# Second feed-forward of an encoder block: chunks 5 and 8 move from plain token chunks into block-product pairs

## The chip, the cores and the metric

The kernel runs on one core of one Trainium2 chip. Its time is the device time of one execution in microseconds (us). The core's engines run side by side, each with its own in-order queue: TensorE (PE in the profile, its weight loads PEld), VectorE (DVE), ScalarE (ACT), GpSimd (POOL) and SyncE (SP). SP and POOL issue the transfers of this case.

## The reference

The block works on 256 tokens of width 1024 in float32: a feed-forward, a mixer of two branches (a gated recurrence and an attention), a read of a memory of 256 tokens, and a second feed-forward. Only the second feed-forward is touched:

```python
D_MODEL, SEQ, D_FF = 1024, 256, 2816

def swiglu(h, w_in, w_down):
    gate, up = jnp.split(h @ w_in, 2, axis=-1)
    return (jax.nn.silu(gate) * up) @ w_down

h = rmsnorm(x, ffn2_pre_g[l])
x = x + 0.5 * rmsnorm(swiglu(h, ffn2_w_in[l], ffn2_w_down[l]), ffn2_post_g[l])
```

## The kernel before, in words

**Splitting.** Every float32 matrix product is made of three products of reduced-precision parts. A block of weights (128 partitions x 1024 elements, 512 KB, "a weight block" below) is loaded by SP into a `raw` buffer. ScalarE casts it to the reduced type (`hi`, line 153 or 173), VectorE subtracts to get the rest (`lo`, line 155 or 174), and TensorE sums hi x hi, hi x lo and lo x hi. There are four `raw` buffers, four buffers of the tag `extra` (the tiles `sraw`), and eight each of `hi` and `lo`.

**Chunks.** `ffn` cuts the 2816 hidden columns into 11 chunks (0 to 10) of 256; with gate and up a chunk has 512 columns and four weight blocks. The 256 tokens are two halves of 128. A token chunk (`act_tok`) multiplies each half of the tokens with the four blocks: 24 matmuls of 128x512 a half, 48 a chunk, and eight instructions of split work on VectorE and ScalarE (four casts, four subtractions).

**Pairs.** `act_pair` takes two neighbouring chunks c and c+1 as a 2x2 block product (two token halves, two halves of the contraction, two chunks) and computes it with seven block products of 12 matmuls in place of eight. The sums of the token blocks are made once (`pair_inputs`, tiles `sx`). The weight sums are made per pair. In order, the products are: W00 (tile `sums`); then `sums` + W01 (tile `both`); then `sums` + W11; then W11 alone (tile `raw`); then `both` = W01 + W11; then W10 alone; last `sums` + W10. Here Wkn is the half k of the contraction and the chunk c+1-n, and each is two weight blocks, so a pair makes 14 casts and 14 `lo` subtractions. The sums on VectorE are `add` (line 596, two instructions a sum, three sums). The fourth sum, W01 + W11, is made by an accumulating transfer that POOL issues (line 569), for the pairs named in `FETCHED`. Two PSUM banks (`b1`, `b4`) gather several products each, and ScalarE copies intermediate states out (`vw` at line 617, `pc` at 630, `vw` at 638, `pc` at 648). VectorE combines them into the four results (`c01` 645, `c11` 651, `c00` 661, the last straight from the bank), each followed by ScalarE's silu (`sg`, 450) and VectorE's product (`at`, 453 or 455).

**Down products.** The results are transposed on TensorE (line 445, four transposes a chunk), split into `act`, and multiplied with two weight blocks of the second matrix (`down`, 12 matmuls a token half, 24 a chunk), summed over all chunks in four banks (`acc`). Pairs take the down products of earlier chunks between their own products; the last three chunks' down products (8, 9, 10) stand at the end, 72 matmuls:

```python
downs = [(i, h) for i in range(done, min(c, NFF - STAG - 1)) for h in range(2)]   # NFF = 11, STAG = 3
...
while done < (NFF - STAG if last == NFF - 1 else min(c - 1 - (c + 1 in pairs), NFF - STAG - 1)):
```

**Order.** The tables at the head of the file say which chunks are token chunks (`TOKS`), where pairs begin (`PAIRS`) and which pairs use the accumulating transfer (`FETCHED`). In the second feed-forward chunks 0 and 1 come first, then 2 as a token chunk, the pair 3-4, token chunk 5, the pair 6-7, token chunk 8, and the pair 9-10. A framework's scheduler puts the program into one in-order list per engine, and sets the waits. The first feed-forward has the pairs 4-5 and 6-7 next to each other, then token chunk 8 and the pair 9-10. When two pairs follow each other, the casts and subtractions for the second product of the later one are held until the last silu of the earlier (`last_silu`).

Of the kernel before, what the change touches and what calls it, by code (L numbers as in the profile page):

```python
# [32 lines left out]

STAG = 3

TOKS = {"f1_in": (3, 8), "f2_in": (2, 5, 8)}

PAIRS = {"f1_in": (4, 6, 9), "f2_in": (3, 6, 9)}

L_ACT = 21  # L40
L_F1 = 24
# [11 lines left out]
M_T = (103, 115)  # L53
M_O = (126, 130)

FETCHED = {"f1_in": (4, 6, 9), "f2_in": (3, 6, 9)}
R_AT = (66, 130, 188, 252, 286, 332)

FG = 3
# [26 lines left out]
def block_kernel(ctx: ExitStack, tc: tile.TileContext, wts, head_in, gf_in, x_in, mem_in, memT_in, cols, rows, fbias, masks, out):  # L86
# [340 lines left out]
    def ffn(w_in, w_dn, X, r2, n_tok, i_row, first_half, second_half=None):  # L427
# [20 lines left out]
        def act_evac(ps, c, h, r=None, q=None):  # L448
            sg = sp.tile([P, FC], F32, tag="c1", name=nm("sg"), bufs=7)
            silu = S.activation(sg, ps[:, :FC], AF.Silu, scale=r2[h] if r is None else r).ins  # L450
            a = sp.tile([P, FC], F32, tag="c1", name=nm("at"), bufs=7)
            if q is None:
                v = V.tensor_tensor(out=a, in0=ps[:, FC:], in1=sg, op=ALU.mult)
            else:
                v = V.scalar_tensor_tensor(out=a, in0=ps[:, FC:], scalar=q, in1=sg, op0=ALU.mult, op1=ALU.mult)
            evs.append((silu, v.ins))
            ats[c, h] = a
            if h == 1:
                late.append(c)
            return silu  # L460
# [110 lines left out]
        def act_pair(c, between):  # L571
            sx, q, more_parts = pairs_in

            def of(n):
                return lambda kk: (sx[n][:, 0, kk], sx[n][:, 1, kk])
# [4 lines left out]
            def splits(t):  # L580
                u = []
                for r in t:
                    p = parts_of()
                    split(p[0], p[1], r)
                    u.append(p)
                return u
# [7 lines left out]
            def add(t, o):  # L594
                for x, y in zip(t, o):
                    V.tensor_tensor(out=x, in0=x, in1=y, op=ALU.add)  # L596

            def product(ps, stat, u, start):
                for kk in range(4):
                    ah, al = stat(kk)  # L600
                    wh, wl = blk(u, kk)
                    for i, (x, y) in enumerate(((ah, wh), (ah, wl), (al, wh))):
                        MM(ps, x, y, start=start and kk == 0 and i == 0, stop=kk == 3 and i == 2, skip_group_check=not start)
# [16 lines left out]
            add(sums, both)  # L620
            if c in FETCHED[w_in]:
                for j in range(2):
# [17 lines left out]
            product(b4, of("baed"), splits(raw), False)  # L640
            if c not in FETCHED[w_in]:
                add(both, raw)
# [43 lines left out]
        last_silu = []  # L686
        pairs, pairs_in = PAIRS[w_in], None
        for c in range(n_tok):
# [25 lines left out]
        for c in range(n_tok, NFF):  # L714
# [17 lines left out]
            elif c == 2 and first_half:  # L732
                n = len(log)
                (outs,) = act_first((c,), mm)
                for h in range(2):
                    flush(n + L_ACT + 24 * h)
                    act_evac(outs[h], c, h)
            elif c in TOKS[w_in]:
                n = len(log)
# [1073 lines left out]
```

## Time and profile before

| | |
|---|---|
| time, median of 3 runs (range) | 767.17 us (767.07 to 767.82) |
| the profiled execution | 767.82 us |
| its span, first to last instruction | 765.6 us |
| first product of the pair 3-4 to the last of the pair 9-10 | about 618 to 736 us |
| down products of the chunks 8, 9, 10 | about 742 to 759 us |

In the rows, a window's line gives the stretch (us from the span's start), its length, each engine's busy time with its count of instructions, TensorE's granted clock, the DMA engines' busy share and GB/s. A row of a timeline gives start and duration in us, engine, line, operation, tiles (output, arrow, inputs), the count of merged instructions, and in brackets the idle time before and what ended it. "SPq" is SP's queue.

### The profile page before, as it was taken

The page shows a single profiled execution, that of the slowest core. Times are in us where ns is not written, and L with a number is a line of the kernel's source. Part 1 is how long each engine was busy: PE and PEld are TensorE (multiplying, and loading weights), DVE is VectorE, ACT ScalarE, POOL GpSimd, SP SyncE. Part 2 cuts the span into 40 slices and gives each one's busy share as a digit, 9 for nine tenths or more (in the row PEclk, how much of TensorE's full clock was granted, in tenths as well). Part 3 has the DMA queues.
Part 4 walks back from the last instruction along what each step waited for, and adds up shares of the span by engine and source line. Part 5 has one row for each costly group of instructions (what it writes and reads, how often), then busy time and mean ns, then how long its engine had stood idle before and what let it go on. Part 6 is the DMA issues. An engine that isn't in the chain of part 4 may idle for free.

```text
span 765.6 us, 11756 instructions
## 1 busy us (share of the span) xinstructions
PE 756.7 (99%) x4302; PEld 642.8 (84%) x4302; DVE 664.4 (87%) x982; ACT 521.2 (68%) x841; POOL 33.0 (4%) x56
## 2 busy tenths in 40 slices
PE   9999999999999999999999999999999999999996
PEld 8888888888888998898888888888887888888885
DVE  6799998988678898888689899999979899997973
ACT  8667576688774659667666755875968566675762
POOL 0000000000000100200001000001000100000000
PEclk9999999999999999999999999999999999999999
DMA  9778777674745545835668955586386837868641
GB/s 350 235 259 245 214 239 275 182 252 167 233 158 149 185 137 183 284 128 182 189 220 245 267 183 186 175 286 131 114 291 191 257 108 257 236 222 269 176 131 55
DMA packets 47146, 157.88 MB, mean 206 GB/s; under 512 B 5385, under 2 KB 9105, under 8 KB 47089
## 3 DMA queue, kind: packets, MB, share of 16 engines
q1 hardware_dynamic: 43168, 144.83, 55.5%
q0 software_dynamic: 3488, 11.94, 8.7%
q8 instruction: 33, 0.54, 0.3%
q10 hardware_dynamic: 432, 0.37, 0.2%
q14 instruction: 25, 0.20, 0.1%
HBM read 156.06 MB, written 1.06 MB: 205 GB/s over the span
## 4 chain that ended last, share of the span: by engine, by line
PE 85%; DVE 8%; ACT 2%; DMA 2%; issue 1%; DVEq 0%; ACTq 0%
PE mm L100 45%; PE acc L100 33%; PE tr L100 5%; DVE lo L155 2%; DMA raw<-in_wts_dram 2%; PE tr L445 1%; DVE lo L174 1%; ACT hi L153 1%; PE tr L385 1%; DVE xs L421 1%; DVE sraw L1393 1%; DMA head<-in_head_dram 0%; DVE post L416 0%; DVE sx L174 0%; DVE qm L1578 0%
## 5 line engine op out<-in xcount | busy, mean ns | idle before, releaser
L155 DVE TENSOR_TENSOR lo<-raw,hi 128x1024 fp32r<-128x1024 f32 (+1 forms) x188 | 222.3, 1199 | 29.5 <-ACT hi L153 26.2
L153 ACT CAST hi<-raw 128x1024 fp32r<-128x1024 f32 (+1 forms) x188 | 190.9, 1033 | 50.3 <-DMA raw<-in_wts_dram 29.7
L100 PE MATMUL mm<-hi,hlT 128*128 128x512 f32 (+1 forms) x632 | 191.6, 382 | 0.0
L100 PEld LDWEIGHTS mm<-hi,hlT 128*128 128x128 f32 x632 | 116.7, 188 | 20.2
L100 PE MATMUL mm<-lo,hlT 128*128 128x512 f32 (+1 forms) x316 | 119.1, 381 | 0.0
L100 PE MATMUL acc<-hi,act 128*128 128x512 f32 x352 | 113.6, 390 | 0.0
L173 ACT CAST hi<-sraw 128x1024 fp32r<-128x1024 f32 x80 | 83.3, 1052 | 33.9 <-DVE sraw L596 15.6
L174 DVE TENSOR_TENSOR lo<-sraw,hi 128x1024 fp32r<-128x1024 f32 x80 | 96.1, 1221 | 3.8 <-ACT hi L173 3.4
L100 PE MATMUL mm<-hi,sx 128*128 128x512 f32 x280 | 90.8, 391 | 0.0
L100 PEld LDWEIGHTS acc<-hi,act 128*128 128x128 f32 x352 | 66.2, 188 | 13.4
L100 PE MATMUL acc<-lo,act 128*128 128x512 f32 x176 | 69.5, 395 | 0.0
L100 PEld LDWEIGHTS mm<-lo,hlT 128*128 128x128 f32 x316 | 59.3, 188 | 10.0
L100 PEld LDWEIGHTS mm<-hi,sx 128*128 128x128 f32 x280 | 52.5, 188 | 10.9
L100 PE MATMUL acc<-hlT,hi 128*128 128x512 f32 x240 | 60.7, 394 | 0.0
L100 PE MATMUL mm<-lo,sx 128*128 128x512 f32 x140 | 54.9, 392 | 0.0
L100 PEld LDWEIGHTS acc<-hlT,hi 128*128 128x128 f32 x240 | 43.1, 189 | 7.7 <-DVE hlT L373 0.2
L174 DVE TENSOR_TENSOR lo<-raw,hi 128x1024 fp32r<-128x1024 f32 x32 | 38.6, 1221 | 2.1 <-ACT hi L173 2.0
L173 ACT CAST hi<-raw 128x1024 fp32r<-128x1024 f32 x32 | 33.1, 1053 | 8.5 <-issue 3.1
L100 PEld LDWEIGHTS acc<-lo,act 128*128 128x128 f32 x176 | 33.1, 188 | 6.4
L100 PE MATMUL acc<-lo,hT 128*128 128x512 f32 x96 | 37.8, 393 | 0.0
L100 PE MATMUL acc<-hi,hT 128*128 128x512 f32 x96 | 37.7, 392 | 0.1
L100 PE MATMUL acc<-hi,lT 128*128 128x512 f32 x96 | 37.3, 391 | 0.0
(329 smaller groups left out, 1232.4 us busy)
## 6 DMA issues: line engine op xcount, KB each, us to landing
raw<-in_wts_dram SPq DMA_DIRECT2D x215, 512.0 KB, 4.6
sraw<-in_wts_dram SPq DMA_DIRECT2D x32, 512.0 KB, 6.6
sraw<-in_wts_dram POOLq DMA_DIRECT2D x20, 512.0 KB, 5.9
raw<-in_gf_dram SPq DMA_DIRECT2D x12, 344.0 KB, 3.7
head<-in_head_dram SPq DMA_DIRECT2D x7, 392.0 KB, 6.4
grow<-in_rows_dram SPq DMA_DIRECT2D x4, 512.0 KB, 7.6
xs<-in_x_dram SPq DMA_DIRECT2D x2, 512.0 KB, 7.6
cb<-cd POOLq DMA_DIRECT2D x2, 512.0 KB, 4.9
```

The lines of the kernel that those rows point to most:

```text
L100: log.append(PE.matmul(*args, **kw).ins)
L153: casts.append(S.copy(h, r).ins)
L155: los.append(V.tensor_tensor(out=l, in0=r, in1=h.bitcast(F32), op=ALU.subtract).ins)
L173: a = S.copy(hi, src)
L174: b = V.tensor_tensor(out=lo, in0=src, in1=hi.bitcast(F32), op=ALU.subtract)
L385: PE.transpose(blocks[-1][1], src(kb), ident)
L421: summed = V.scalar_tensor_tensor(out=xh, in0=ts[a // 512][:, a % 512 : (b - 1) % 512 + 1], scalar=r, in1=xh, op0=ALU.mult, op1=ALU.add)
L445: PE.transpose(trv[:, j, h * P : (h + 1) * P], ats[c, h][:, j * P : (j + 1) * P], ident)
L1393: V.tensor_tensor(out=x, in0=x, in1=y, op=ALU.add)
```

## The change

Three entries of the tables change, all for the second feed-forward:

```diff
-TOKS = {"f1_in": (3, 8), "f2_in": (2, 5, 8)}
+TOKS = {"f1_in": (3, 8), "f2_in": (2,)}

-PAIRS = {"f1_in": (4, 6, 9), "f2_in": (3, 6, 9)}
+PAIRS = {"f1_in": (4, 6, 9), "f2_in": (3, 5, 7, 9)}
...
-FETCHED = {"f1_in": (4, 6, 9), "f2_in": (3, 6, 9)}
+FETCHED = {"f1_in": (4, 6, 9), "f2_in": (3, 5, 7, 9)}
```

Chunks 3 to 10 become the pairs 3-4, 5-6, 7-8, 9-10, one right behind the other. Two token chunks (96 matmuls, eight casts and eight `lo` subtractions) go; one pair (84 matmuls, 14 casts, 14 subtractions, six adds, three combinations, two accumulating transfers) comes. Through `downs` the down products are dealt out anew: chunks 3 and 4 go into the pair 5-6, chunks 5 and 6 into the pair 7-8, and none into the pair 9-10, which had chunk 6 before.

VectorE, last pair: the rows between the `lo` subtractions of the fifth product and those of the last (before: the last product's two, `lo_1606` and `lo_1608`, stand ahead of `c01`). Before:

```order
L174 TENSOR_TENSOR lo_1606_7571<-sraw_1550_7354,hi_1605_7570 128x1024
L174 TENSOR_TENSOR lo_1608_7575<-sraw_1551_7356,hi_1607_7574 128x1024
L155 TENSOR_TENSOR lo_1614_7604<-raw_1612_7602,hi_1613_7603 128x1024
L645 TENSOR_TENSOR c01_1585_7504<-mm_1569_7416,vw_1556_7364 128x512
L155 TENSOR_TENSOR lo_1617_7616<-raw_1615_7614,hi_1616_7615 128x1024
L453 TENSOR_TENSOR at_1587_7508<-c01_1585_7504,sg_1586_7506 128x256
L155 TENSOR_TENSOR lo_1621_7647<-raw_1619_7645,hi_1620_7646 128x1024
```

The same place now (the last product's are `lo_1622` and `lo_1624`):

```order
L645 TENSOR_TENSOR c01_1601_7535<-mm_1586_7466,vw_1578_7431 128x512
L174 TENSOR_TENSOR lo_1615_7574<-raw_1612_7569,hi_1614_7573 128x1024
L453 TENSOR_TENSOR at_1603_7539<-c01_1601_7535,sg_1602_7537 128x256
L174 TENSOR_TENSOR lo_1617_7578<-raw_1613_7570,hi_1616_7577 128x1024
L651 TENSOR_TENSOR c11_1608_7562<-pc_1579_7432 128x512
L596 TENSOR_TENSOR sraw_1572_7421<-sraw_1572_7421,raw_1612_7569 128x1024
L455 SCALAR_TENSOR_TENSOR at_1610_7566<-c11_1608_7562,q_1317_6336,sg_1609_7564 128x256
L661 TENSOR_TENSOR c00_1618_7595<-vw_1578_7431,tr_1611_7568 128x512
L596 TENSOR_TENSOR sraw_1573_7423<-sraw_1573_7423,raw_1613_7570 128x1024
L453 TENSOR_TENSOR at_1620_7599<-c00_1618_7595,sg_1619_7597 128x256
L174 TENSOR_TENSOR lo_1622_7602<-sraw_1572_7421,hi_1621_7601 128x1024
L174 TENSOR_TENSOR lo_1624_7606<-sraw_1573_7423,hi_1623_7605 128x1024
```

The last product's subtractions now stand behind the combinations of the first three results, and all eight subtractions of line 155 that followed them in part before now come after them.

ScalarE, last pair: the copies `vw` and `pc` out of the banks, and the casts of the third and fourth product (before `hi_1577`, `hi_1579` and `hi_1581`, `hi_1583`; now `hi_1593`, `hi_1595` and `hi_1597`, `hi_1599`). Before:

```order
L173 CAST hi_1577_7463<-sraw_1550_7354 128x1024
L450 ACTIVATE sg_1548_7350<-mm_1547_7325,facs_85 128x256
L617 COPY vw_1556_7364<-mm_1558_7366 128x512
L173 CAST hi_1579_7467<-sraw_1551_7356 128x1024
L173 CAST hi_1581_7484<-raw_1575_7457 128x1024
L173 CAST hi_1583_7488<-raw_1576_7458 128x1024
L173 CAST hi_1588_7510<-sraw_1552_7358 128x1024
L630 COPY pc_1557_7365<-mm_1569_7416 128x512
```

Now:

```order
L617 COPY vw_1578_7431<-mm_1580_7433 128x512
L173 CAST act_1509_7147<-tr_1585_7455 128x512
L630 COPY pc_1579_7432<-mm_1586_7466 128x512
L173 CAST hi_1593_7494<-sraw_1572_7421 128x1024
L173 CAST hi_1595_7498<-sraw_1573_7423 128x1024
L173 CAST hi_1597_7515<-raw_1591_7488 128x1024
L173 CAST hi_1599_7519<-raw_1592_7489 128x1024
```

The copy `pc`, which waits for the end of the second product, stood behind the casts of the third and fourth and now stands ahead of them.

SP, behind the loads of the sixth product of the pair 3-4 (`raw_1419`, `raw_1420`): before, four loads of chunk 5 and then the pair 6-7's `sums` and `both`:

```order
L567 DMA raw_1420_6779<-in_wts_dram 128x1024
L151 DMA raw_1437_6855<-in_wts_dram 128x1024
L151 DMA raw_1440_6861<-in_wts_dram 128x1024
L151 DMA raw_1443_6867<-in_wts_dram 128x1024
L151 DMA raw_1446_6873<-in_wts_dram 128x1024
L567 DMA sraw_1455_6943<-in_wts_dram 128x1024
```

Now the pair 5-6's `sums` (`sraw_1435`, `sraw_1436`), and its `both` (`sraw_1437`, `sraw_1438`) after four more loads:

```order
L567 DMA raw_1420_6779<-in_wts_dram 128x1024
L567 DMA sraw_1435_6853<-in_wts_dram 128x1024
L567 DMA sraw_1436_6855<-in_wts_dram 128x1024
L151 DMA raw_1449_6898<-in_wts_dram 128x1024
L151 DMA raw_1452_6910<-in_wts_dram 128x1024
L567 DMA raw_1460_6956<-in_wts_dram 128x1024
L567 DMA raw_1461_6957<-in_wts_dram 128x1024
L567 DMA sraw_1437_6857<-in_wts_dram 128x1024
```

The `sums` of the next pair moved up to stand right behind the last raw loads of the pair 3-4.

## The prediction

> **What bounds the kernel now.** I read the page's first part, then the waits of TensorE alone, then the windows of the second feed-forward, and last the timelines of VectorE, ScalarE and SP around the pairs. First the page's busy time, the one wait of TensorE between 590 us and the end, and the stretch from the end of the pair 3-4's VectorE work to the last product of the pair 9-10:
>
> ```profile
> PE 756.7 (99%) x4302; PEld 642.8 (84%) x4302; DVE 664.4 (87%) x982; ACT 521.2 (68%) x841; POOL 33.0 (4%) x56
> ...
> PE tr L445 <- DVE at L455: 0.3, 1, 0.3
> ...
> 646.07:725.06 78.99, 78.99 (x361) 65.38 (x361) 72.10 (x76) 52.45 (x65) 3.38 (x4) 1.00 0.75 236
> 688.00:700.00 12.00, 12.00 (x59) 9.94 (x58) 8.45 (x11) 6.43 (x10) 0.00 (x0) 1.00 0.92 333
> ```
>
> TensorE never waits here but for 0.3 us, so it is the bound. VectorE is close behind it: 72.1 of 79.0 us. Much of its rest lies where token chunk 8 begins (8.45 of 12 us busy). The change takes those token chunks away. So the question is whether VectorE can follow a pair-only stretch.
>
> **TensorE's side.** A block product of 12 matmuls takes 2.72 us in the chain of waits, so 0.2267 us a matmul; four transposes take 0.44 us:
>
> ```profile
> 626.79 2.72 PE acc L100 x12
> ...
> 649.00 6.59 PE mm L100 x29
> 655.59 0.44 PE tr L445 x4
> ...
> 739.93 19.09 PE acc L100 x84
> 759.02 0.02 issue
> ```
>
> Two token chunks of 48 matmuls go and 84 matmuls come: 12 x 0.2267 = 2.7 us less, all on the path if nothing else binds. The pair 3-4's last product starts at 649.00 and ends 651.7 (12 of the 29 matmuls). From there to the start of the last product of the pair 9-10 TensorE has now 240 matmuls of 20 products, 96 of down products and 20 transposes: 336 x 0.2267 + 5 x 0.44 = 78.4 us, to 730.1. Before it was 348 matmuls, 81.1 us, to 732.8; the trace has 732.87 (next fence), so the count holds.
>
> **VectorE's side.** Up to 646.07 its list is the same as before. Start to start, a 1024-wide instruction takes 2.27/2 = 1.135 us, a 512-wide 0.60, `at` of line 453 0.33 and of line 455 0.39:
>
> ```profile
> 620.57 0.69 DVE L543 TENSOR_TENSOR ss<-xf 128x512 f32<-128x512 f32 x1
> 621.17 0.69 DVE L542 TENSOR_TENSOR ss<-ss,xf 128x512 f32<-128x512 f32 x1
> ...
> 645.68 0.49 DVE L455 SCALAR_TENSOR_TENSOR at<-c,q,sg 128x256 f32<-128x256 f32 x1
> 646.07 1.23 DVE L155 TENSOR_TENSOR lo<-raw,hi 128x1024 fp32r<-128x1024 f32 x1
> ...
> 662.10 2.36 DVE L174 TENSOR_TENSOR lo<-sraw,hi 128x1024 fp32r<-128x1024 f32 x2
> 664.37 0.42 DVE L453 TENSOR_TENSOR at<-mm,sg 128x256 f32<-128x256 f32 x1
> 664.70 2.36 DVE L596 TENSOR_TENSOR sraw<-sraw,raw 128x1024 f32<-128x1024 f32 x2
> ...
> 725.06 1.22 DVE L174 TENSOR_TENSOR lo<-sraw,hi 128x1024 fp32r<-128x1024 f32 x1
> ...
> 732.87 0.39 PE L100 MATMUL mm<-hi,sx 128*128 128x512 f32 x1
> 736.05 0.39 PE L100 MATMUL acc<-hi,act 128*128 128x512 f32 x1
> ```
>
> The last product (the matmul at 732.87) needs the `lo` that VectorE starts at 725.06. Before, VectorE's list from 646.07 up to and with that `lo` holds 55 wide instructions, 10 of 512, seven and three `at`: 62.4 + 6.0 + 2.3 + 1.2 = 71.9 us. It was done at 726.2, after 80.1 us: 8.2 us of idle, and then 6.7 us of reserve before TensorE came. Now the list up to the last product's first `lo` (`lo_1622`) holds 67 wide, 16 of 512, seven and six `at`: 76.0 + 9.6 + 2.3 + 2.3 = 90.3 us, so 18.4 more. The reserve of 8.2 + 6.7 = 14.9 us is used up and 3.5 us are left: without any idle VectorE delivers at 736.4, and the last product starts at 736.4 in place of 732.87. The 2.7 us that TensorE saves become waiting: 736.4 - 730.1 = 6.3 us, nearly all in the last pair, which has no down products between its own any more.
>
> **Idle that VectorE cannot shed.** In a pair it waits at times for ScalarE's casts, which stand behind a copy that waits for TensorE. The pairs 6-7 and 9-10 lose 0.38 + 0.64 and 0.66 + 0.19 us to that; the copy `pc` in pair 9-10 waited for its product:
>
> ```profile
> 667.43 2.36 DVE L174 TENSOR_TENSOR lo<-sraw,hi 128x1024 fp32r<-128x1024 f32 x2 [0.38 <-ACT hi L173]
> 682.38 1.23 DVE L155 TENSOR_TENSOR lo<-raw,hi 128x1024 fp32r<-128x1024 f32 x1 [0.64 <-ACT hi L153]
> ...
> 707.82 1.23 DVE L174 TENSOR_TENSOR lo<-sraw,hi 128x1024 fp32r<-128x1024 f32 x1 [0.66 <-ACT hi L173]
> ...
> 718.97 0.59 ACT L630 COPY pc<-mm 128x512 f32<-128x512 f32 x1 [0.26 <-PE mm L100]
> ...
> 726.47 1.23 DVE L174 TENSOR_TENSOR lo<-sraw,hi 128x1024 fp32r<-128x1024 f32 x1 [0.19 <-ACT hi L173]
> ```
>
> Now `pc` stands ahead of the third product's casts in the last pair: end of the second product, copy (0.5), cast (1.05), then `lo`. That is a ring through three engines with nothing to fill it but two adds. From nothing to 3 x 1.02 = 3.1 us over three pairs; I take 1.2, one pair's worth and a little, since where VectorE is the late engine most other waits have gone by.
>
> **The tail.** Behind the last product stand 24 down matmuls of chunk 7 and 72 of the chunks 8 to 10, on six weight blocks; the same matmuls as before. What changes is when the blocks are split:
>
> ```profile
> 730.59 4.57 DMA raw<-in_wts_dram
> ...
> 735.26 1.05 ACT L153 CAST hi<-raw 128x1024 fp32r<-128x1024 f32 x1 [1.40 <-DMA raw<-in_wts_dram]
> ...
> 739.35 1.22 DVE L155 TENSOR_TENSOR lo<-raw,hi 128x1024 fp32r<-128x1024 f32 x1
> ```
>
> Before, the last block's `lo` ended at 740.6, with the final 84 matmuls beginning at 739.93 and that block wanted some 6 us later. Now eight `lo` stand behind the last product's two. There are four `raw` buffers, so the last four blocks load only as the first four are split. A cycle is 4.57 + 1.05 + 1.22 = 6.8 us. With the last product at 737.6 (736.4 + 1.2) the first four splits end at 739.9, 741.0, 742.7 (behind an `act` split and an `at`) and 744.2, so the last four blocks are ready at 746.7, 747.9, 749.6 and 751.1. TensorE ends the last product at 740.8 (732.87 to 736.05 was 3.18), chunk 7 at 746.6, and wants the third to sixth tail block at 748.0, 748.7, 749.4 and 750.0. The last one is 1.1 us late. Nothing at the low end; at the high end 3.6, if loads take the 7.1 us of the `sraw` row below in place of 4.57. I take 0.9.
>
> **The rest at nothing.** Silu and copies on ScalarE (52 of 79 us busy) hide under VectorE. The two new accumulating transfers cost POOL two issues of 0.85 us. They have four products' time to land, 6.5 us by their row; without that cover the fifth product waits.
>
> ```profile
> sraw<-in_wts_dram SPq DMA_DIRECT2D x12, 512.0 KB, 7.1
> sraw<-in_wts_dram POOLq DMA_DIRECT2D x6, 512.0 KB, 6.5
> ...
> L569 POOL DMA_DIRECT2D sraw<-in_wts_dram x12: 839/850/887, 54.3 to 705.3; - x12
> ...
> 656.00:666.00 10.00, 10.00 (x46) 8.24 (x45) 10.00 (x12) 4.67 (x8) 1.69 (x2) 1.00 0.78 175
> ```
>
> **Sum.** 3.5 + 1.2 + 0.9 = 5.6 us. The profiled execution took 767.82 (span 765.6 and 2.2 around it), 0.65 above the median; it becomes 773.4. On the median that is 767.17 + 5.6 = 772.8. Ends: 3.5 gives 770.7, and 3.5 + 3.1 + 3.6 = 10.2 gives 777.4.
>
> **Rivals.** *TensorE stays the bound; faster.* For it speaks the first feed-forward, with the pairs 4-5 and 6-7 side by side and no wait of TensorE:
>
> ```profile
> 57.50:119.97 62.47, 62.47 (x283) 51.72 (x282) 59.94 (x61) 42.23 (x52) 1.69 (x2) 1.00 0.78 242
> ...
> 71.39 3.27 SPq L567 DMA_DIRECT2D sraw<-in_wts_dram  x2
> ...
> 73.09 1.22 DVE L174 TENSOR_TENSOR lo<-sraw,hi 128x1024 fp32r<-128x1024 f32 x1
> ```
>
> Then 767.17 - 2.7 = 764.4. Against it: there 283 matmuls and transposes cover two pairs, here 356 cover three, and VectorE was at 59.9 of 62.5 even so. It decides if VectorE's list falls below 84.1 us (730.1 - 646.07), seven per cent under my count. Chance 0.04; a near balance, within 0.2% (1.5 us, what a measurement can tell), 0.02.
>
> *TensorE's clock falls in the waits.* After the last matmul the granted clock held, then halved:
>
> ```profile
> 759.00:762.00 3.00, 0.01 (x1) 0.00 (x0) 2.03 (x6) 1.54 (x5) 0.00 (x0) 1.00 0.00 0
> 762.00:762.50 0.50, 0.00 (x0) 0.00 (x0) 0.50 (x2) 0.00 (x0) 0.00 (x0) 0.84 0.05 18
> 762.50:763.00 0.50, 0.00 (x0) 0.00 (x0) 0.21 (x1) 0.00 (x0) 0.00 (x0) 0.50 1.01 347
> ```
>
> So some 3.3 us after the last matmul (759.02). The 6.3 us of waiting fall in several pieces, the longest about 3 us ahead of the last product. If one piece is long enough, that product's 12 matmuls run at half rate: 2.7 us more, 775.5. Chance 0.14. The Trainium skill (TensorE: Matmul & The Clock Gate, Part 1: The HAM clock gate) says that an idle window of about 3.4 us halves the clock, and about as long a busy one restores it; by that rule, an estimate, the loss would be about 1.7 us, and the trace's 3.3 us agrees.
>
> *The hand-over between pairs is laid bare.* If the next pair's `sums` loaded only when the last product's blocks are split (`lo` ending 645.8), then 7.1 us of load and 1.05 of cast come before VectorE goes on, about 6 us at each of three hand-overs: 779 for one, 791 for all. Against it: SP's list has these loads behind the sixth product's, and in the first feed-forward they left at 71.39, while VectorE was still at the fifth product's blocks (73.09). Chance 0.06.
>
> *The accumulating transfers come late.* If a busy VectorE held POOL back by one wide instruction for each of the two in three pairs, 6 x 1.2 = 7.2 us more: 780. Against it, POOL's issues spread only from 0.839 to 0.887 us, two of them in ten microseconds in which VectorE was busy throughout. Chance 0.02. The Trainium skill (SBUF — State Buffer, SBUF: two separate sides) warns that VectorE's two-port modes lock GpSimd out and starve such transfers of descriptors; the trace shows no sign of it here.
>
> **Numbers.** Forecast 0.72, clock 0.14, hand-over 0.06, transfers 0.02, faster 0.04, same 0.02. Faster is 0.04, same 0.02, slower 0.94. Forecast and clock hold 0.86; the range is their ends: 770.0 (770.7 less the runs' spread of 0.7) to 777.2, two tenths under the forecast's upper end, whose three worst terms hardly meet.
>
> **What would show it.** In the changed profile TensorE should wait for the first time in the second feed-forward, some 6 to 8 us in all, mostly for `lo` of line 174 and in the pair 9-10. VectorE should be busy over 95% from 646 to 737, and the last product should start near 737.6. TensorE waiting for `lo` of line 155 in the final down products shows the tail. I am wrong if VectorE idles several us at a hand-over, if the granted clock falls before 760, or if TensorE still does not wait.

## The result, and the profile after

The changed kernel takes 775.44 us (median of four, 774.67 to 778.85), the kernel before 767.5 beside it: ratio 1.0112, 95% interval 1.0081 to 1.0144, so 1.1% slower. Forecast were 772.8 us and a range of 770.0 to 777.2. The profiled execution took 774.89 us, with a span of 773.1 against 765.6.

The page's busy time, then the waits of TensorE from 590 us on and those of VectorE from 645 to 740 (in total, times, longest), and a window that reaches from the start of VectorE's list (645.44, 0.63 earlier than before) to the end of the last product's first `lo`:

```profile
PE 757.8 (98%) x4290; PEld 642.1 (83%) x4290; DVE 679.7 (88%) x997; ACT 528.8 (68%) x851; POOL 34.9 (5%) x58
...
PE mm L100 <- DVE lo L174: 2.9, 3, 2.0
PE mm L100 <- ACT hi L173: 2.6, 2, 1.6
PE tr L445 <- DVE at L455: 2.2, 3, 1.3
...
DVE sraw L596 <- DMA sraw<-in_wts_dram: 1.3, 2, 1.0
DVE lo L174 <- ACT hi L173: 0.6, 2, 0.4
DVE lo L155 <- ACT hi L153: 0.2, 1, 0.2
...
645.44:739.32 93.88, 86.22 (x384) 69.21 (x383) 91.54 (x98) 62.55 (x81) 5.08 (x6) 1.00 0.68 205
```

TensorE now waits 7.7 us, where it had waited 0.3. VectorE is busy for 91.5 of 93.9 us: the late engine. Now TensorE's timeline: the third product of the pair 9-10 (first and second matmul), the last product (the same two), and the first down matmul behind it; for comparison the last product's second matmul before:

```profile
723.77 0.49 PE L100 MATMUL mm<-hi,sx 128*128 128x512 f32 x1 [1.62 <-ACT hi L173]
725.03 0.50 PE L100 MATMUL mm<-lo,sx 128*128 128x512 f32 x1 [0.77 <-DVE lo L174]
...
736.93 0.49 PE L100 MATMUL mm<-hi,sx 128*128 128x512 f32 x1 [0.95 <-ACT hi L173]
739.39 0.50 PE L100 MATMUL mm<-lo,sx 128*128 128x512 f32 x1 [1.97 <-DVE lo L174]
...
743.98 0.48 PE L100 MATMUL acc<-hi,act 128*128 128x512 f32 x1
```

```profile
733.09 0.39 PE L100 MATMUL mm<-lo,sx 128*128 128x512 f32 x1
```

And the granted clock (the figure behind POOL's) around the last product:

```profile
736.00:739.00 3.00, 0.49 (x1) 0.19 (x1) 3.00 (x5) 2.33 (x4) 0.00 (x0) 1.00 0.56 187
...
740.00:741.00 1.00, 1.00 (x6) 0.68 (x5) 1.00 (x2) 1.00 (x2) 0.00 (x0) 0.88 0.51 205
741.00:742.00 1.00, 1.00 (x6) 1.00 (x5) 1.00 (x2) 0.85 (x1) 0.00 (x0) 0.50 0.00 0
...
744.00:745.00 1.00, 1.00 (x5) 0.83 (x4) 0.80 (x2) 0.76 (x2) 0.00 (x0) 0.91 0.80 168
```

From 736 to 739 TensorE ran a single matmul. From about 740.8 to 744.2 it had half its clock (0.88 of a us at 1 or a half puts the fall at 740.76; the rise follows in the same way from 0.91). So the last product was late, and then slow: from its second matmul to the first down matmul 739.39 to 743.98 = 4.59 us, before 733.09 to 736.05 = 2.96.

**Where 7.5 us of span come from.** Whole executions are shifted against each other by up to three us ahead of the place of the change. So I count from one instruction ahead of it, the second `ss` addition of line 542 (621.17 before):

```profile
620.52 0.68 DVE L542 TENSOR_TENSOR ss<-ss,xf 128x512 f32<-128x512 f32 x1
```

The last product's second matmul comes 739.39 - 620.52 = 118.87 us behind it, before 733.09 - 621.17 = 111.92: 6.95 later. The half clock adds 4.59 - 2.96 = 1.63. From the first down matmul to the end it is 773.1 - 743.98 = 29.12, before 765.6 - 736.05 = 29.55 (before, 0.3 us of wait for `at` lay in it): 0.43 less. The whole execution lay 0.65 earlier. 6.95 + 1.63 - 0.43 - 0.65 = 7.5.

Below, "ss to down" is the time from this addition to the first down matmul behind the last product: 736.05 - 621.17 = 114.88 before, 743.98 - 620.52 = 123.46 after, so 8.6 more. TensorE's 12 matmuls less would give 114.88 - 2.72 = 112.2.

### The profile page after: what moved, and what is told of

Its sections match the earlier page's. It is cut to its first block, busy times and chain, and to the rows that moved or that the text cites. A ratio compares the mean times of both kernels' runs of the same rounds, so it can differ in the third digit from the quotient of the medians.

```text
span 773.1 us, 11772 instructions
## 1 busy us (share of the span) xinstructions
PE 757.8 (98%) x4290; PEld 642.1 (83%) x4290; DVE 679.7 (88%) x997; ACT 528.8 (68%) x851; POOL 34.9 (5%) x58
## 4 chain that ended last, share of the span: by engine, by line
PE 84%; DVE 8%; DMA 3%; ACT 3%; issue 2%; DVEq 0%; ACTq 0%; SPq 0%
PE mm L100 38%; PE acc L100 37%; PE tr L100 5%; DVE lo L174 3%; DVE sraw L596 2%; DMA sraw<-in_wts_dram 1%; DMA raw<-in_wts_dram 1%; ACT hi L173 1%; PE tr L445 1%; DVE lo L155 1%; PE tr L385 1%; ACT pm L1649 1%; ACT hi L153 0%; PE tr L1265 0%; DVE at L455 0%
## 5 line engine op out<-in xcount | busy, mean ns | idle before, releaser
L155 DVE TENSOR_TENSOR lo<-raw,hi 128x1024 fp32r<-128x1024 f32 (+1 forms) x180 | 212.3, 1196 | 24.9 <-ACT hi L153 21.6
L153 ACT CAST hi<-raw 128x1024 fp32r<-128x1024 f32 (+1 forms) x180 | 182.3, 1032 | 44.5 <-DMA raw<-in_wts_dram 29.0
L100 PE MATMUL mm<-hi,hlT 128*128 128x512 f32 (+1 forms) x576 | 175.4, 381 | 0.0
L100 PEld LDWEIGHTS mm<-hi,hlT 128*128 128x128 f32 x576 | 106.3, 188 | 18.1
L173 ACT CAST hi<-sraw 128x1024 fp32r<-128x1024 f32 x90 | 93.2, 1051 | 37.1 <-DVE sraw L596 22.7
L174 DVE TENSOR_TENSOR lo<-sraw,hi 128x1024 fp32r<-128x1024 f32 x90 | 107.8, 1219 | 2.9 <-ACT hi L173 2.6
L100 PE MATMUL mm<-lo,hlT 128*128 128x512 f32 (+1 forms) x288 | 108.2, 380 | 0.0
L100 PE MATMUL mm<-hi,sx 128*128 128x512 f32 x320 | 104.6, 393 | 2.6 <-ACT hi L173 2.6
L100 PE MATMUL mm<-lo,sx 128*128 128x512 f32 x160 | 63.7, 398 | 2.9 <-DVE lo L174 2.9
L100 PEld LDWEIGHTS mm<-lo,sx 128*128 128x128 f32 x160 | 30.3, 190 | 9.9 <-DVE lo L174 4.0
```

The lines of the kernel that those rows point to most:

```text
L100: log.append(PE.matmul(*args, **kw).ins)
L153: casts.append(S.copy(h, r).ins)
L155: los.append(V.tensor_tensor(out=l, in0=r, in1=h.bitcast(F32), op=ALU.subtract).ins)
L173: a = S.copy(hi, src)
L174: b = V.tensor_tensor(out=lo, in0=src, in1=hi.bitcast(F32), op=ALU.subtract)
```

## The experiments

Theory: VectorE's list has become longer than TensorE's work, and the time follows its length. Rivals: the hand-over between neighbouring pairs; the order of ScalarE's copies and casts; the clock. The median of the kernel before was 766.99 to 768.17 us on the chips used, so the ratios count.

### Is it the length of VectorE's list?

**One addition less in each pair.** The sums' own third block is no longer added (it is loaded and used):

```diff
 product(b0, of_x(1), splits(raw), True)
-add(sums, raw)
+if w_in != "f2_in":
+    add(sums, raw)
```

> The changed kernel, in which the four pairs of the second feed-forward leave out the addition of the sums' own third block (it is still loaded); its result is not the reference's. Two 1024-wide additions fewer in each of four pairs, three of them inside the stretch from 646 us to the last product: VectorE's list 90.3 - 6 x 1.135 = 83.5 us, done at 729.6, with the 3.5 us of idle that the changed kernel showed about 733. Theory VectorE is the late engine: the last product starts about 730 to 733 in place of 736.9, TensorE waits under 3 us in all, the clock holds: 764.5 to 768, some 8 us faster than the changed kernel. Rival, the hand-over and ScalarE's copies set the time (not the length of VectorE's list): the waits stay, and the time is at most 2 us better than the changed kernel's, 773 or more. Rival, the clock alone: it stays at 775 if it falls.

**Two additions less.** The same, and the second neighbour's block is not added either:

```diff
 raw = raws(1, 1)
-add(sums, raw)
+if w_in != "f2_in":
+    add(sums, raw)
```

> As the run without the last addition, and the addition of the second neighbour's block to the sums is left out as well; its result is not the reference's. VectorE's list 90.3 - 12 x 1.135 = 76.7 us, below TensorE's 78.4 us. Theory VectorE is the late engine: TensorE is the bound again, waits under 1 us, and the program takes the kernel before's time less the 2.7 us of 12 matmuls, 764.5 on a median of 767.2. Rival, hand-over between pairs or the order of the copies: TensorE still waits several us in the pair 9-10, and the time is 768 or more.

Measured: one addition less 769.26 us, ratio 1.0027 (1.0012 to 1.0043); two less 766.84 us, ratio 0.9984 (0.9971 to 0.9998). TensorE's waits with one less, the `ss` addition and the first down matmul; then the same for two less:

```profile
PE mm L100 <- DVE lo L174: 1.2, 1, 1.2
PE tr L445 <- DVE at L455: 1.2, 1, 1.2
PE acc L100 <- DVE lo L155: 0.7, 1, 0.7
...
621.54 0.68 DVE L542 TENSOR_TENSOR ss<-ss,xf 128x512 f32<-128x512 f32 x1
737.17 0.40 PE L100 MATMUL acc<-hi,act 128*128 128x512 f32 x1
```

```profile
PE acc L100 <- DVE lo L155: 0.5, 1, 0.5
PE acc L100 <- ACT hi L153: 0.3, 1, 0.3
...
621.55 0.68 DVE L542 TENSOR_TENSOR ss<-ss,xf 128x512 f32<-128x512 f32 x1
734.65 0.39 PE L100 MATMUL acc<-hi,act 128*128 128x512 f32 x1
...
646.07:736.40 90.33, 90.33 (x413) 74.44 (x411) 78.89 (x86) 67.51 (x86) 5.06 (x6) 1.00 0.70 210
```

The ss to down is 115.63 and 113.10 us, against 123.46. Taking the 1.63 us of half clock out, the first addition left out (eight instructions behind `ss`, 9.1 us) gave 6.2, and the second 2.5 more, until TensorE no longer waits in the pairs (90.33 of 90.33 busy) and VectorE has time to spare (78.9). In this second run `ss` itself came 0.9 us earlier against TensorE's own matmuls than in the changed kernel; counted by TensorE, the stretch is the 112.2 us of its work alone. The hand-over is refuted as a cause: in the second run VectorE still waits 2.0 us for a load at the hand-over between the first two of the four pairs, and TensorE does not notice. The order of ScalarE's copies is not refuted by these runs, since it moved with the edit: `pc` of the last pair stands between the third product's casts in the first (721.30, casts at 720.35 and 722.09) and behind them in the second (720.92). For this rival the changed kernel's own trace gives the bound: VectorE waits for ScalarE's casts for 0.8 us in its whole list, 0.36 of them behind `pc`.

Both runs are slower than I expected (769.3 against at most 768, 766.8 against 764.5). In each, TensorE waits 0.7 to 0.8 us for weight blocks in the final down products (the second of eight in the first run, the last two in the second): the tail of the prediction, which the changed kernel itself does not show. So a list shorter than TensorE's work would have brought the change a gain of 0.2% (up to 0.3%), not the 2.7 us of its matmuls.

**The other direction.** The pairs 5-6 and 7-8 without an accumulating transfer, two additions more on VectorE in each:

```diff
-FETCHED = {"f1_in": (4, 6, 9), "f2_in": (3, 5, 7, 9)}
+FETCHED = {"f1_in": (4, 6, 9), "f2_in": (3, 9)}
```

> The changed kernel, with the pairs 5-6 and 7-8 making the sum W01 + W11 on VectorE instead of by the accumulating transfer (four wide adds more on VectorE, two megabytes less by accumulating transfers but the same loads). Theory VectorE (its list up to the last product's subtractions sets when the last product can start): 4 x 1.135 = 4.5 us later, so about 780 us, TensorE's waits longer by as much. Rival transfers (the accumulating transfers and the loads at the hand-over between pairs hold the kernel up): 775.4 us or less, since two of four accumulating transfers are gone.

Measured: 778.25 us, ratio 1.014 (1.0122 to 1.0158). The waits of TensorE, `ss` and first down matmul, and a window from `ss` to the end of the last product's first `lo`:

```profile
PE mm L100 <- DVE lo L174: 4.0, 4, 2.1
PE mm L100 <- ACT hi L173: 3.2, 4, 1.2
...
622.02 0.69 DVE L542 TENSOR_TENSOR ss<-ss,xf 128x512 f32<-128x512 f32 x1
745.83 0.40 PE L100 MATMUL acc<-hi,act 128*128 128x512 f32 x1
...
622.02:742.69 120.67, 112.41 (x496) 89.33 (x494) 120.28 (x129) 81.19 (x105) 1.69 (x2) 1.00 0.57 185
```

The times decide nothing here: the ratio's interval overlaps the changed kernel's (1.0112, and 1.0133 in a second measurement below), and neither the 780 us of the theory nor the rival's 775.4 or less came. The traces do. In the same stretch of the changed kernel VectorE is busy for 116.5 of 118.8 us, here for 120.3 of 120.7: 3.8 us more work, 1.9 us less idle time, and the last product's first `lo` is ready 1.9 us later. So the longer list made the last product later, by less than the 4.5 us of four additions, since VectorE no longer waits for loads and casts. In this execution the clock did not fall, which hides the difference in the time. The same stretch in all five traces:

| | stretch (us) | VectorE busy in it | ss to down |
|---|---|---|---|
| before | 105.1 | 98.2 | 114.88 |
| changed | 118.8 | 116.5 | 123.46 |
| one addition less in each pair | 111.7 | 105.8 | 115.63 |
| two additions less in each pair | 108.5 | 96.6 | 113.10 |
| four additions more | 120.7 | 120.3 | 123.81 |

With one addition less VectorE already has 5.9 us of idle time, and TensorE still waits 2.7 us ahead of the first down matmul; so the time does not follow the list's length alone once the list is near TensorE's work. Leaving an addition out also takes a link out of the chain from load to cast to `lo`. That the length of this chain, and not of the list, made the changed kernel late is excluded by its own trace: a chain that holds VectorE up would show as idle time of VectorE, and there are only 2.3 us of that in 93.9.

### Does the hand-over between neighbours cost?

Three pairs as before, but two of them side by side (3-4 and 5-6), with the token chunks 7 and 8 behind them; the work is the kernel before's in another order:

```diff
-TOKS = {"f1_in": (3, 8), "f2_in": (2,)}
+TOKS = {"f1_in": (3, 8), "f2_in": (2, 7, 8)}
-PAIRS = {"f1_in": (4, 6, 9), "f2_in": (3, 5, 7, 9)}
+PAIRS = {"f1_in": (4, 6, 9), "f2_in": (3, 5, 9)}
```

> Three pairs as before, but the pairs 3-4 and 5-6 next to each other, then token chunks 7 and 8, then the pair 9-10: the same count of every instruction as the kernel before, with one hand-over between neighbouring pairs. Theory VectorE: the total of VectorE's list is unchanged and the token chunks give the reserve back before the last pair, so 767 to 768 us, no wait of TensorE of more than 1 us. Rival transfers (a hand-over itself costs some 2 to 3 us, three of them in the changed kernel): 769.5 to 771 us.

Measured: 769.27 us, ratio 1.0015 (1.0005 to 1.0025). TensorE's only wait from 590 us on:

```profile
PE tr L445 <- DVE at L455: 0.9, 1, 0.9
```

Two pairs side by side cost about 1 us, where I had expected none (767 to 768 us) and the rival 2 to 3. That is far from the six us a hand-over that a rival of the prediction named.

### What does the clock add?

**Matmuls to fill the last wait.** Ten matmuls whose result is not used, ahead of the last product of the pair 9-10:

```diff
+if c + 1 == NFF - 1 and w_in == "f2_in":
+    for _ in range(10):
+        PE.matmul(b4, X.hi(0, 0, P), X.both(0), start=True, stop=True, skip_group_check=True)
```

> The changed kernel with ten matmuls that feed nothing (128x512 each, 2.3 us) put ahead of the last product of the pair 9-10, where TensorE waits 2.9 us. They write a bank that has been read. Theory clock (the two waits there, with one matmul between, let the granted clock fall to a half for 3.3 us): the clock stays at 1.00 until the end, the last product takes 3.0 instead of 4.6 us, and the kernel is 1.0 to 1.6 us faster than the changed one, 773.8 to 774.4 us; the last weight blocks of the tail may take a few tenths back. Rival (the clock costs nothing, since VectorE or the tail's blocks set the end): 775.4 us or up to 1 us more.

**Real work in the last pair.** The down products of chunk 6 go from the pair 7-8 into the pair 9-10:

```diff
-downs = [(i, h) for i in range(done, min(c, NFF - STAG - 1)) for h in range(2)]
-done = max(done, min(c, NFF - STAG - 1))
+upto = min(c, NFF - STAG - 1) - (c == 7 and w_in == "f2_in")
+downs = [(i, h) for i in range(done, upto) for h in range(2)]
+done = max(done, upto)
```

> The changed kernel with chunk 6's down products (24 matmuls, 5.4 us) moved from the pair 7-8 into the pair 9-10, where the kernel before had them. All instructions are the same. Theory VectorE and clock: the last product cannot start sooner (VectorE's list ahead of it is the same), but the waits are spread over the last two pairs and the clock does not fall, so 1.0 to 1.6 us faster than the changed kernel, 773.8 to 774.4 us. Rival (TensorE's work was badly dealt out, and the missing cover in the last pair is what cost the time): 5 us faster, about 770 us.

Measured, on the same chip: fill 776.43 us, ratio 1.0111 (1.0097 to 1.0126); work moved 775.06 us, ratio 1.0087 (1.0073 to 1.01). Both lie above the 773.8 to 774.4 us that I expected, though the kernel before takes 768.17 us on this chip and thus 0.7 more than beside the changed kernel; the moved work is far from its rival's 770. The profiled execution of the filled kernel kept its clock and had a span of 771.8, 1.3 below the changed kernel's; three of the other four had spans of 774.7 to 775.5 at mean clocks of 0.994 to 0.995. So this run alone decided nothing: filling one wait left the other one, at the third product. That led to a second fill.

**Both waits filled, beside the changed kernel again.** Eight idle matmuls more ahead of the third product, into a bank that is free there:

```diff
+if c + 1 == NFF - 1 and w_in == "f2_in":
+    spare = trp()
+    for _ in range(8):
+        PE.matmul(spare, X.hi(0, 0, P), X.both(0), start=True, stop=True, skip_group_check=True)
```

> The changed kernel with matmuls that feed nothing in two waits of TensorE in the pair 9-10: eight ahead of the third product (1.8 us, where it waits 2.4) and ten ahead of the last (2.3 us, where it waits 2.9). Theory clock: no stretch of the last pair is long enough any more, the mean granted clock is 0.997 to 0.998 in all runs, none of them is above 775 us, and the median is 1 to 3 us below the changed kernel's. Rival (the clock costs nothing): the same median as the changed kernel or up to 1 us more, and no narrower spread.

> The changed kernel itself once more, as the measure for the three beside it on the same chip: 774.5 to 777 us against 767 to 768.5 us of the kernel before. Theory VectorE and clock: where a run's mean granted clock is lower (0.994 to 0.995 against 0.997 to 0.998), it is 2 to 4 us longer, since a half-rate stretch of 3.3 us costs 1.6 us and there are several waits that can set one off. Without a part of the clock the runs do not order by it.

Measured: changed kernel 776.93 us, ratio 1.0133 (1.0112 to 1.0153); both waits filled 775.57 us, ratio 1.0107 (1.0094 to 1.0121). The two intervals overlap, so the 1.4 us between the medians are not clear of noise. Of the four filled executions three lie above the 775 us that none should have passed; they spread over 2.1 us, the five of the changed kernel over 4.9. The profiled execution of the changed kernel (span 777.8), four windows, `ss` and first down matmul; then one window, `ss` and first down matmul of the filled one (773.7):

```profile
725.00:726.00 1.00, 0.34 (x1) 0.34 (x2) 1.00 (x2) 1.00 (x2) 0.00 (x0) 0.52 0.00 0
730.00:732.00 2.00, 2.00 (x6) 1.52 (x6) 1.29 (x2) 1.24 (x2) 0.00 (x0) 0.53 0.80 293
...
742.00:743.00 1.00, 0.09 (x1) 0.09 (x1) 1.00 (x2) 1.00 (x2) 0.00 (x0) 0.55 0.50 107
748.00:749.00 1.00, 1.00 (x4) 0.76 (x3) 1.00 (x2) 0.40 (x2) 0.00 (x0) 0.53 0.83 209
...
621.60 0.69 DVE L542 TENSOR_TENSOR ss<-ss,xf 128x512 f32<-128x512 f32 x1
748.62 0.54 PE L100 MATMUL acc<-hi,act 128*128 128x512 f32 x1
```

```profile
720.00:750.00 30.00, 28.05 (x126) 22.23 (x125) 28.94 (x32) 23.07 (x30) 0.85 (x1) 1.00 0.56 162
...
621.73 0.69 DVE L542 TENSOR_TENSOR ss<-ss,xf 128x512 f32<-128x512 f32 x1
743.81 0.40 PE L100 MATMUL acc<-hi,act 128*128 128x512 f32 x1
```

Here the changed kernel's clock was halved twice, at the waits of the third product (725.0 to 731.9 us) and at those of the last (742.1 to 748.9), for 6.8 us each time, by the windows in which it falls and rises, with 0.50 between them; in the execution of the first section the same waits had led to one fall only, of 3.4 us. With both filled the clock stays at 1.00. The ss to down is 122.08 us (one wait filled, in the execution without a fall: 121.36), which is 7.2 and 6.5 more than before. So 6.5 to 7.2 of the changed kernel's 8.6 us are VectorE's lateness, and the clock adds the rest: 1.6 us in one execution, and some five in the other (127.02 us). On the median it may be about 1.4 us (776.93 - 775.57). The runs do not order by the mean clock throughout: at 0.997 the changed kernel's spans reach from 773.1 to 776.8, so something else varies by up to three us too. In its profiled execution, moving real work kept the clock as well; that kernel has the lowest ratio of the four-pair kernels that compute everything. One window, and the last product's second matmul:

```profile
715.00:750.00 35.00, 31.11 (x137) 24.43 (x136) 33.35 (x35) 24.80 (x32) 1.70 (x2) 1.00 0.63 180
...
738.45 0.50 PE L100 MATMUL mm<-lo,sx 128*128 128x512 f32 x1 [2.09 <-DVE lo L174]
```

With its `ss` at 621.18 that matmul comes 117.27 us behind it, 1.6 earlier than in the changed kernel and 5.4 later than before; TensorE still waits 2.09 us there. How much of the 1.6 is the other order of the work, and how much chance, one profile doesn't tell.

The Trainium skill (TensorE: Matmul & The Clock Gate, Part 1: The HAM clock gate) says that the window in which the chip looks at TensorE's activity, about 3.4 us, runs freely and is not set off by the kernel's own work. That agrees with equal waits that here halve the clock in one execution and not in the other, and with stretches of half clock of 3.4, 6.8 and 6.8 us, one or two such windows. Its rule of no idle gaps above about 3.4 us is not enough here: the longest single wait was 1.97 us, with one matmul between it and a wait of 0.95 us.

### Can the additions go elsewhere?

**A second accumulating transfer in all four pairs.** GpSimd's queue adds the block of the last addition too:

```diff
+if w_in == "f2_in":
+    for j in range(2):
+        more(sums[j], c, 1, 0, j, ALU.add)
...
-add(sums, raw)
+if not (w_in == "f2_in"):
+    add(sums, raw)
```

> The changed kernel with one more block sum of each pair of the second feed-forward made by an accumulating transfer: the last (sums + W10), issued by POOL right after the third product's subtractions, in place of two adds of VectorE a pair. VectorE's list from 645 us to the last product's subtractions falls by six wide adds, 6.8 us, to 83.5 us; TensorE's work in that stretch is 78.4 us. Theory VectorE: the last product starts some 6.5 us sooner, the clock holds, and the kernel comes to 766 to 768 us, near the kernel before or just under it. Rival transfers: a second accumulating transfer a pair makes the waits longer, 776 us or more.

> The kernel before (three pairs) with the same second accumulating transfer in place of two VectorE adds a pair. Theory VectorE: TensorE did not wait there, so nothing is won, within 0.5 us of the kernel before; what relief of VectorE is worth shows only where it is the late engine. Rival (any relief of VectorE helps): 2 us or more faster than before. If the transfers themselves cost something, it shows here alone: slower by that.

The second of these expectations is for the same edit in the kernel before, with its three pairs. Measured: in four pairs 778.7 us, ratio 1.0157 (1.0141 to 1.0173); in three pairs 768.34 us, ratio 1.0014 (1.0005 to 1.0024). I had expected a gain from the first, and its ratio is above the changed kernel's (1.0112 and 1.0133), though the intervals touch. The second is 0.14% slower, about 1 us, where I had expected no difference above 0.5 us: that may be what the transfers cost where VectorE is not late. The first one's waits of VectorE and of ScalarE from 600 to 745 us and the raw loads' row of the DMA view from 600 to 740 (count, KB each, median us from issue to landing); then that row of the changed kernel:

```profile
DVE lo L174 <- ACT hi L173: 11.5, 7, 3.4
...
ACT hi L173 <- DMA raw<-in_wts_dram: 9.0, 3, 4.2
...
raw<-in_wts_dram SPq DMA_DIRECT2D x32, 512.0 KB, 7.1
```

```profile
raw<-in_wts_dram SPq DMA_DIRECT2D x31, 512.0 KB, 4.6
```

From `ss` to the last product's first `lo` VectorE works 10.9 us less than in the changed kernel, but stands idle for 11.2 us in place of 2.3. The plain loads of weight blocks land in 7.1 us in place of 4.6, ScalarE waits for them, and VectorE for ScalarE. In its trace two accumulating transfers leave at 664.05 and 665.66, just ahead of the sixth product's raw loads; the first of these left at 666.19 and took 7.8 us to land, where the same load of the changed kernel (663.51), with no accumulating transfer ahead of it, took 3.3. The changed kernel shows the same where it does have two ahead: the load behind them, at 653.19, took 7.5 us. Over the runs the median of the raw loads from 600 to 740 us goes up, roughly, with the number of accumulating transfers there: 4.2 us with 4 (the run with four additions more on VectorE), 4.5 and 4.6 with 6, 4.5 to 5.1 with 8, 5.2 with 10, 5.1 with 12 (three pairs), 7.1 with 16. What is not separated is whether the accumulating slows them or only the bytes: this run fetches the sixth product's blocks twice, 32.2 MB in place of 27.9 in these 140 us.

**Only in the last pair,** where no next pair loads:

```diff
+if w_in == "f2_in" and c == 9:
+    for j in range(2):
+        more(sums[j], c, 1, 0, j, ALU.add)
...
-add(sums, raw)
+if not (w_in == "f2_in" and c == 9):
+    add(sums, raw)
```

> The changed kernel, and in the pair 9-10 alone the last addition is made by a second accumulating transfer in place of VectorE. In all four pairs this was slower than the changed kernel, and ScalarE waited for raw loads. Theory that these transfers hold up the loads of the next pair: the pair 9-10 has no next pair, its DMA share is 0.43 to 0.56 in place of 0.68, so here the two additions are saved, 2.3 us off VectorE's list, and the last product starts about 2 us earlier: 772 to 774 (1.5 to 3 us below the changed kernel). Rival, the transfer's own landing (some 6 us in place of 2.3 us of VectorE) is what costs: the sums come late, TensorE waits for `hi` of the sums' product, and the time is the changed kernel's or more, 776 to 779.

Measured: 775.9 us, ratio 1.011 (1.0095 to 1.0125), as the changed kernel: nearer the rival, and no gain. GpSimd's second issue of the two, the link of the chain that follows from it, and ScalarE's cast behind it:

```profile
727.22 0.84 POOL L569 DMA_DIRECT2D sraw<-in_wts_dram  x1 [0.29 <-DVE lo L174]
...
727.22 9.45 DMA sraw<-in_wts_dram
...
736.75 1.04 ACT L173 CAST hi<-sraw 128x1024 fp32r<-128x1024 f32 x1 [3.71 <-DMA sraw<-in_wts_dram]
```

The transfer can only leave when the sums have been split for the product before, and it landed 9.45 us later, where VectorE had needed 2.3. ScalarE's queue then holds VectorE up too: the copy `pc` for the second result stands behind that cast (at 737.70), and VectorE waits 3.56 us for it.

**The addition on GpSimd:**

```diff
-add(sums, raw)
+for x, y in zip(sums, raw):
+    (G if w_in == "f2_in" else V).tensor_tensor(out=x, in0=x, in1=y, op=ALU.add)
```

> The changed kernel with the last addition of the sums' own block done by GpSimd in place of VectorE in the four pairs; the result is the reference's. VectorE's list is 83.5 us as in the run that leaves the addition out. Theory that the length of VectorE's list sets the time, and GpSimd works beside it: 765 to 769 if GpSimd's additions take no longer than some 3 us each. Rival, GpSimd is slow or the two hold each other up: VectorE's instructions that stand beside an addition of GpSimd grow longer than 1.14 us, or `hi` of the sums' product waits for GpSimd, and the time is 775 or more.

Measured: 783.69 us, ratio 1.0219 (1.0187 to 1.0252): the slowest of all, the rival. Part of that is the clock: it was halved in three stretches (means of 0.66 from 650 to 655 us, 0.83 from 690 to 700 and 0.83 from 720 to 730). Two additions of GpSimd, and VectorE's subtractions at the same time:

```profile
733.38 2.38 POOL L659 TENSOR_TENSOR sraw<-sraw,raw 128x1024 f32<-128x1024 f32 x1 [8.17 <-DVE lo L174]
736.93 3.31 POOL L659 TENSOR_TENSOR sraw<-sraw,raw 128x1024 f32<-128x1024 f32 x1 [1.17 <-DVE lo L174]
```

```profile
733.54 3.31 DVE L174 TENSOR_TENSOR lo<-sraw,hi 128x1024 fp32r<-128x1024 f32 x1 [0.24 <-ACT hi L173]
736.77 4.56 DVE L174 TENSOR_TENSOR lo<-raw,hi 128x1024 fp32r<-128x1024 f32 x2
```

The subtraction that starts at 733.54, with GpSimd's addition already running, ends at 736.85: 1.1 us after GpSimd's end at 735.76. The addition that starts at 736.93, behind a subtraction, takes longer by that subtraction's rest. The eight additions took GpSimd 3.6 us each in the mean. So the two take turns, and an addition that meets VectorE costs it some 2.1 us (3.31 in place of 1.22) where it would have spent 1.135 itself. The Trainium skill (SBUF — State Buffer, SBUF: two separate sides) says just this, that the two engines' shared port pair is an exclusive lock which the one that starts first holds for its whole instruction; the trace agrees.

None of the kernels that compute the reference's result beats the kernel before.

## Why the prediction was right, and where its sizes were off

**The mechanism held.** VectorE became the late engine, and TensorE's saved 2.7 us became waiting: VectorE is busy for 91.5 of the 93.9 us that end with the `lo` for which the last product waits. The two runs that leave additions out show it too: with the list well below TensorE's work the waits in the pairs are gone. Of the signs named ahead, TensorE waits 7.7 us (6 to 8) and VectorE is busy 97.5% (over 95). The waits are mostly in the pair 9-10 (1.62 + 0.77 + 0.95 + 1.97 = 5.3 us), but less than half of them are for `lo`; the rest stands at `hi` and `at`. Most of it goes back to VectorE in turn, but not all: the cast that ends the 1.62 us at the third product follows the copy `pc`, which waits for the end of the second product as the prediction said, while VectorE's addition had been ready some 0.4 us before the cast began (721.04 + 1.22 = 722.26 against 722.67):

```profile
722.18 0.59 ACT L630 COPY pc<-mm 128x512 f32<-128x512 f32 x1 [1.95 <-PE mm L100]
```

TensorE never waited for `lo` of line 155 in the final down products.

**Two signs went against it.** The last product began at 736.93, and 737.6 was forecast, but the near match is luck: the matmul at 732.87, by which the forecast went, takes `hi` and does not wait for `lo`. The second matmul does, and the `lo` that was to be ready at 737.6 was ready at 739.34, 2.4 us late when counted from `ss`. And the clock fell at 740.8 us: a granted clock that falls before 760 was named as a sign of being wrong. The path through VectorE was right; that the clock would hold was not.

**"+3.5", the list: 4.7 in place of 3.5.** The list itself was counted exactly (67 wide instructions, 16 of 512, seven and six `at`), and it grew by 18.2 us of busy time where 18.4 were forecast. Too large was the reserve ahead of it. Over the stretch of the old list VectorE was busy for 73.3 us, and not 71.9:

```profile
646.07:726.28 80.21, 80.21 (x366) 66.38 (x366) 73.32 (x76) 53.67 (x66) 3.38 (x4) 1.00 0.75 237
```

The price of 1.135 us holds for instructions in a row, while one ahead of a wait, even a short one, takes its full 1.22; each list has some 14 of them. So the idle time before was 6.9 us and not 8.2, and 18.2 - 6.9 - 6.6 = 4.7 us were left.

**"Idle that VectorE cannot shed, +1.2": 2.3**, inside its bounds of 0 to 3.1. But the cause is in the main another than the casts behind `pc`, which cost 0.36 us in the last pair. More than half of it, 1.3 us, is the wait for the next pair's `both` load:

```profile
681.31 1.22 DVE L596 TENSOR_TENSOR sraw<-sraw,sraw 128x1024 f32<-128x1024 f32 x1 [1.02 <-DMA sraw<-in_wts_dram]
```

That is a small piece of the hand-over which the prediction had as a rival at 6 us each and gave 0.06. The term's evidence was thin from the start: of the four waits before, only the 0.38 and the 0.19 us stand behind a copy; at the other two the cast itself waited for TensorE. The two terms make 4.7 + 2.3 = 7.0, and the trace has 6.95.

**"The tail, +0.9": not seen in the changed kernel, and yet real.** With the clock kept, TensorE does wait for blocks of the tail: 0.2 to 0.4 us with waits filled, 0.7 to 0.8 in the runs with fewer or more additions. That in the profiled execution of the changed kernel the half-rate product gave these blocks the time fits, but is not shown. One reading in this part was off, without a bearing on the sum: the `lo` that ended at 740.6 before was the seventh of the eight tail blocks; the last one started at 741.13 and ended at 742.4. (And the rival's 730.1 - 646.07 is 84.0, not 84.1; nothing hangs on it.)

**The clock, a rival at 0.14: it came.** It is no alternative to the forecast but lies on top of it. The prediction counted only one wait's length ("about 3 us ahead of the last product") and took the fall for unlikely. The place was right, the loss 1.63 us in the first profile against 2.7 forecast, since the fall came only 1.4 us into the product; in the second it came at the third product too. An estimate by the Trainium skill's rule (TensorE: Matmul & The Clock Gate, Part 1: The HAM clock gate) had been 1.7. That the median of 775.44 lies beside this rival's 775.5 is luck: the rival added 2.7 us of clock to 5.6 us of lateness and tail, and the trace has 1.6 and 7.0.

So 772.8 was 2.6 us low against 775.44. In the profiled span the step was 7.5 us against the forecast 5.6: the list missed 1.2, the idle time 1.1 and the clock 1.6; the tail, forecast and not seen, gave 0.9 back, and 1.1 came from the earlier start of the whole execution (0.65) and the shorter end (0.43).

**What stays open.** Why the same waits halve the clock in one execution and not in the next is not settled by these runs. Nor is it shown whether the accumulating or the added bytes delay the raw loads.

## What to carry to other kernels

When work moves from an engine that bounds the time to the next one, add up that engine's list up to the instruction that the bound engine waits for; with its idle time and lead as the reserve, that sum gave the sign and most of the size. Add the list from start to start, and count an instruction ahead of a wait at its full length. Where the bound engine starts to wait in several pieces close together, put the clock into the sum and not among the rivals.

## What the runs showed of the hardware that was not expected

- At waits of 0.95 and 1.97 us with one matmul between them TensorE's clock was halved, for 3.4 us in one execution and 6.8 in another; at waits of 1.62 and 0.76 us it was halved in the second (6.8 us) and not in the first. With matmuls that feed nothing in these waits it stayed at 1.00 in the profiled execution.
- GpSimd's additions and VectorE's subtractions of two tiles in SBUF took turns: a 128x1024 addition on GpSimd took 2.38 us where it came first, and a subtraction of VectorE that met it 3.31 in place of 1.22.
- More accumulating transfers went with slower plain loads beside them (7.1 in place of 4.6 us median from issue to landing for 512 KB), while GpSimd's issues themselves stayed at about 0.85 us.
